# Inverting the 16x16 diagonal blocks of the delta rule from 4x4 and 8x8 blocks instead of row by row

## The chip, the cores and the metric

The kernel is one program on one core of a Trainium2 chip. The metric is the device time of one execution in microseconds (us); less is better. The engines are named as the profile names them: PE is TensorE (matrix products), DVE is VectorE, ACT is ScalarE, POOL is GpSimd, and SP issues most DMAs.

## The reference, cut to what matters

The program is a first block of two layers, followed by a second block that the change does not touch. A layer adds a feed-forward network, a mixer and another feed-forward network to x. The mixer has three parts: attention over selected keys, RWKV-7 time mixing, and a gated delta rule. The last two are recurrences over the 512 tokens. The reference writes the delta rule in chunks of 64 tokens with a triangular solve:

```
for l in range(DEPTH):                                   # DEPTH = 2
    x = x + 0.5 * swiglu(rms_norm(x, ...), ...)
    p = rms_norm(x, mix_norm[l]) @ w_in[l]
    pa, pb, pc = split_cols(p, GROUP_SPLITS)
    ya = dsa_attention(pa, ...)                          # top-k keys of each query, softmax
    yb, v_first = rwkv7_time_mix(pb, ...)                # 4 heads
    yc = gated_deltanet(pc, ...)                         # 4 heads
    x = x + jnp.concatenate([ya, yb, yc], axis=-1) @ w_out[l]
    x = x + 0.5 * swiglu(rms_norm(x, ...), ...)

# inside gated_deltanet, for each head and each chunk of 64 tokens
lower = jnp.where(strict, einsum('bhncd,bhnsd->bhncs', kb, k) * decay, 0.0)
rhs = jnp.concatenate([v * beta[..., None], kb * jnp.exp(g)[..., None]], axis=-1)
sol = lax.linalg.triangular_solve(eye + lower, rhs, left_side=True, lower=True, unit_diagonal=True)
```

RWKV-7 is written as a scan over tokens in the reference; the kernel gives it the same chunked form with the same solve.

## The kernel before, in words

Each layer's mixer is built by `Mix.__init__`. The projections (tiles `pf`, three matmuls for each fp32 product) feed everything. Four parts then run the chunked recurrence, each for two heads: `r0` and `r1` (RWKV) and `g0` and `g1` (gated delta rule). Each calls `Mix.core()` once, so a layer has four calls and the program eight. Attention stands beside them: the selection of keys (`index`, lines 542 to 544, repeated MAX8 and MATCH_REPLACE on DVE), and `att(t)` for the four tiles t of 128 queries. `att(t)` first rotates the queries (L471, L473) and turns and splits them (`qs`, L486). Then come two groups of four heads. For each head there are two matmuls, a masked maximum on DVE (L612), an exponential on ACT (L617) and a reciprocal (L619). After four heads the weights are turned by PE (`pT`, copied by L626) and multiplied by the values. L633 copies the tile's result out. `att(3)` has the widest scores, 128x512.

The order on each engine is not the order of the code. A scheduler lays out all instructions by streams with a tag and a level (`chain("c", 0)`, `("a", 0)` for the recurrences, `("g", 1)` for attention, `("x", 1)` for the selection, `("w", 2)` for weights); each engine then works through its own queue strictly in that order. The mixer ends with the product by `w_out`, which takes its eight pieces in the order 4, 5, 6, 7 (the recurrences), 0, 1, 2, 3 (attention).

`core()` solves the 64x64 triangular systems in two levels. The blocks G (`GA` for the delta rule, written by L1053) go to DRAM (L654), and their 16x16 diagonal blocks come back with one block on each of 64 partitions (L655): tile `d16`, 256 numbers each. GpSimd sets the identity in `x16`. Then 15 steps follow the rows of the block. Step s multiplies column s below the diagonal with row s of the inverse so far (L663, (15-s)(s+1) numbers) and adds that to all rows below (L665). Each of the 30 instructions needs the one before it. L666 copies the transposed inverse beside it, L667 writes both to DRAM, L672 reads them back in the layout of the 128-partition tiles, and L676 spreads them into block-diagonal tiles X0 and XT0. PE then multiplies (`lv`, L691), with DVE additions (`v`, L701) between the products, `WU` (L709), `qg` (L720), the matrices M (L745) and the eight states S (L759), whose result the part turns into `y` and `yo` (for g0 and g1: L1069, L1071).

Of the kernel before, what the change touches and what calls it, by code (L numbers as in the profile page):

```python
# [14 lines left out]
ALU = mybir.AluOpType  # L15
AX = mybir.AxisListType
# [76 lines left out]
def bc(ap, shape):  # L93
    return ap.to_broadcast(shape)
# [233 lines left out]
class Mix:  # L328
# [310 lines left out]
    def core(self, G, R, KH, RT, PC, extra=None, beta=None):  # L639
# [3 lines left out]
        nc, n, sm = self.nc, self.n, self.sm  # L643
# [5 lines left out]
        dt = n.f("d16")[:64]  # L649
        d16, t16 = dt[:, 0:256].rearrange("p (s t) -> p s t", s=16), dt[:, 256:320]  # L650
# [2 lines left out]
            for e in range(2):  # L653
                q.dma_start(out=rows[th, e], in_=G[th][e][:, :, 0:128])  # L654
        q.dma_start(out=d16, in_=s1[:, 0:2048].rearrange("x (s t) -> x s t", t=128)[:, :, 0:16])  # L655
        x16 = n.f("x16")[:64].rearrange("p (a c) -> p a c", a=2)
        X = x16[:, 0].rearrange("p (r c) -> p r c", r=16)
        nc.gpsimd.memset(x16[:, 0], 0.0)
        nc.gpsimd.memset(x16[:, 0, 0:256:17], 1.0)
        for s in range(15):  # L660
            a, m = 15 - s, s + 1
            tt = t16[:, :a * m].rearrange("p (r c) -> p r c", r=a)
            nc.vector.tensor_mul(out=tt, in0=bc(d16[:, s, s + 1:16].rearrange("p (r o) -> p r o", o=1), [64, a, m]),  # L663
                                 in1=bc(X[:, s:s + 1, 0:m], [64, a, m]))
            nc.vector.tensor_add(out=X[:, s + 1:, 0:m], in0=X[:, s + 1:, 0:m], in1=tt)  # L665
        nc.vector.tensor_copy(out=x16[:, 1].rearrange("p (c r) -> p c r", c=16), in_=X.rearrange("p r c -> p c r"))  # L666
        q.dma_start(out=s2.rearrange("a p c -> p a c"), in_=x16)  # L667
        xs2 = n.f("xs16")
        m16 = n.c("m16").rearrange("p (o g c) -> p o g c", o=1, g=8)
        xs = [xs2[:, a * 128:(a + 1) * 128].rearrange("p (i c) -> p i c", i=8) for a in range(2)]  # L670
        for a in range(2):
# [27 lines left out]
        for _ in range(3):  # L699
            w = self.half("v") if v is R else v  # L700
# [7 lines left out]
        else:  # L708
            prod(XT0, v, lambda h, b: nc.vector.tensor_mul(  # L709
                out=WU[h].rearrange("p (u e) c -> p u e c", e=2), in0=b.rearrange("p (u e) c -> p u e c", e=2),  # L710
                in1=bc(beta[:, 2 * h:2 * h + 2], [128, 2, 2, 128])))

        blocks = [(th, u, e) for th in range(2) for u in range(2) for e in range(2)]
# [14 lines left out]
        for cp in range(2):  # L728
            cs = slice(cp * 64, cp * 64 + 64)
            b = n.bank("bMB")  # L730
            col = lambda a, th, u: slice(a * 256 + (th * 2 + u) * 64, a * 256 + (th * 2 + u) * 64 + 64)
# [3 lines left out]
            for th, u, e in blocks:  # L735
                i = th * 4 + 2 * u + e
# [17 lines left out]
        for c in range(1, 8):  # L754
            nc.tensor.matmul(bY[:, c * 64:c * 64 + 64], lhsT=st(c), rhs=RT[:, c * 64:c * 64 + 64], start=False, stop=(c == 7))
            if c < 7:
                b = n.bank("bS")
# [832 lines left out]
```

## Time and the profile before

| | |
|---|---|
| time, median of 3 runs | 3542.82 us (3540.81 to 3544.31) |
| profiled execution, its time and its span | 3542.9 us, 3541.1 us |
| PE busy | 3414.4 us, 96% of the span |
| DVE busy | 2010.9 us, 57% |
| ACT busy | 1274.9 us, 36% |
| mixer of layer 0, layer 1 | about 375 to 801 us, 1560 to 1990 us |

The span runs from the first to the last instruction of the profiled execution; the 1.8 us between it and that execution's time lie around the program. Busy shares are means over very different stretches: in the feed-forward networks PE has no gap to speak of, and in the last 150 us of each mixer no engine is busy throughout.

### The profile page before, as it was taken

To read this page: it belongs to the slowest core of one execution; us is meant where nothing else is said; L and a number is where in the kernel's file an instruction comes from. 1 tells how busy PE (TensorE), PEld (TensorE's weight loads), DVE (VectorE), ACT (ScalarE), POOL (GpSimd) and SP (SyncE) were. 2 spreads that over 40 slices of the span, in tenths; PEclk is the share of its full clock that TensorE was granted. 3 is DMA by queue.
4 is the path that set the end of the run, shared out by engine and by line. 5 is a ranking of instruction groups with operands and counts; after the bars stand their busy time and mean duration, and the time that the engine had idled before them with its cause. 6 is when DMAs were issued, how large, how long until landed. Compare 5 with 4: busy or idle time off the path is not lost.

```text
span 3541.1 us, 44468 instructions
## 1 busy us (share of the span) xinstructions
PE 3414.4 (96%) x17314; PEld 2801.3 (79%) x17314; DVE 2010.9 (57%) x4364; ACT 1274.9 (36%) x2060; POOL 84.7 (2%) x168
## 2 busy tenths in 40 slices
PE   8999999889999999999998899999999999989999
PEld 7888778668888888887877688888777888778887
DVE  5555688765555555559978555535785332473332
ACT  4332544453332233335344433324563222232321
POOL 0000010000000000001100000000000000000000
PEclk9999999789999999999978999999999999989999
DMA  5346321103335434552210233432202333223332
GB/s 164 119 140 210 112 66 50 30 16 115 123 122 190 152 119 122 192 156 65 52 49 14 84 115 124 131 110 79 78 7 83 96 100 97 69 78 99 97 95 95
DMA packets 329955, 355.73 MB, mean 100 GB/s; under 512 B 41192, under 2 KB 249480, under 8 KB 329616
## 3 DMA queue, kind: packets, MB, share of 16 engines
q1 hardware_dynamic: 328576, 351.03, 32.5%
q8 instruction: 136, 2.23, 0.3%
q10 hardware_dynamic: 1168, 1.85, 0.2%
q14 instruction: 75, 0.61, 0.1%
HBM read 338.68 MB, written 14.16 MB: 100 GB/s over the span
## 4 chain that ended last, share of the span: by engine, by line
PE 89%; DVE 7%; ACT 2%; issue 1%; DMA 1%; POOL 0%; SPq 0%; DVEq 0%; ACTq 0%; POOLq 0%
PE pg L168 13%; PE pg L170 13%; PE pg L169 13%; PE pd L168 8%; PE pd L169 8%; PE pd L170 8%; PE pf L169 2%; PE pf L170 2%; PE pf L168 2%; PE lv L691 2%; PE G L904 1%; PE pt L430 1%; PE pt L431 1%; PE pt L429 1%; DVE wlo L162 1%
## 5 line engine op out<-in xcount | busy, mean ns | idle before, releaser
L162 DVE TENSOR_TENSOR wlo<-wraw,whi 128x1024 fp32r<-128x1024 f32 (+2 forms) x504 | 609.3, 1209 | 958.8 <-ACT whi L161 958.1
L161 ACT CAST whi<-wraw 128x1024 fp32r<-128x1024 f32 (+2 forms) x504 | 524.8, 1042 | 1283.6 <-PE pd L169 505.4
L168 PE MATMUL pg<-xh,whi 128*128 128x512 f32 x2112 | 825.5, 391 | 14.1 <-ACT whi L161 10.6
L170 PE MATMUL pg<-xh,wlo 128*128 128x512 f32 x2112 | 824.0, 390 | 0.0
L169 PE MATMUL pg<-xl,whi 128*128 128x512 f32 x2112 | 823.9, 390 | 0.0
L168 PEld LDWEIGHTS pg<-xh,whi 128*128 128x128 f32 x2112 | 398.1, 189 | 97.0 <-ACT whi L161 10.6
L169 PEld LDWEIGHTS pg<-xl,whi 128*128 128x128 f32 x2112 | 397.9, 188 | 83.1 <-DVE xl L273 0.6
L170 PEld LDWEIGHTS pg<-xh,wlo 128*128 128x128 f32 x2112 | 397.6, 188 | 83.5 <-DVE wlo L162 0.8
L168 PE MATMUL pd<-h,whi 128*128 128x512 f32 x1056 | 410.9, 389 | 0.0
L170 PE MATMUL pd<-h,wlo 128*128 128x512 f32 x1056 | 410.9, 389 | 0.0
L169 PE MATMUL pd<-h,whi 128*128 128x512 f32 x1056 | 410.8, 389 | 0.0
L1106 DVE CUSTOM_DVE_ANT_0 araw<-araw,act 128x512 f32<-128x512 f32 x224 | 148.9, 688 | 145.9 <-DMA araw<-in_ada_w_dram 140.6
L169 PEld LDWEIGHTS pd<-h,whi 128*128 128x128 f32 x1056 | 198.2, 188 | 41.3
L170 PEld LDWEIGHTS pd<-h,wlo 128*128 128x128 f32 x1056 | 198.2, 188 | 41.2
L168 PEld LDWEIGHTS pd<-h,whi 128*128 128x128 f32 x1056 | 198.2, 188 | 40.9
L168 PE MATMUL pf<-xh,whi 128*128 128x512 f32 (+4 forms) x424 | 167.0, 395 | 0.9 <-ACT xh L272 0.9
L169 PE MATMUL pf<-xl,whi 128*128 128x512 f32 (+4 forms) x424 | 167.3, 395 | 0.4 <-DVE xl L273 0.4
L170 PE MATMUL pf<-xh,wlo 128*128 128x512 f32 (+4 forms) x424 | 166.7, 393 | 0.0
L294 ACT ACTIVATE t<-t 128x512 f32<-128x512 f32 x88 | 55.6, 632 | 252.4 <-DVE t L293 250.6
L174 DVE TENSOR_TENSOR h<-t,h 128x512 fp32r<-128x512 f32 x132 | 90.8, 690 | 65.0 <-ACT h L173 64.7
L173 ACT CAST h<-t 128x512 fp32r<-128x512 f32 x132 | 81.8, 620 | 123.6 <-DVE t L296 76.7
L169 PEld LDWEIGHTS pf<-xl,whi 128*128 128x128 f32 (+2 forms) x424 | 79.1, 187 | 17.9 <-DVE xl L273 2.5
(494 smaller groups left out, 4692.8 us busy)
## 6 DMA issues: line engine op xcount, KB each, us to landing
wraw<-in_ffn_w_dram SPq DMA_DIRECT2D x132, 512.0 KB, 3.7
araw<-in_ada_w_dram SPq DMA_DIRECT2D x112, 512.0 KB, 3.5
wraw<-in_ffn_w_gate_dram SPq DMA_DIRECT2D x88, 512.0 KB, 3.8
wraw<-in_ffn_w_up_dram SPq DMA_DIRECT2D x88, 512.0 KB, 4.5
wraw<-in_ffn_w_down_dram SPq DMA_DIRECT2D x88, 512.0 KB, 3.6
wraw<-in_w_in_dram SPq DMA_DIRECT2D x69, 512.0 KB, 3.8
wraw<-in_w_out_dram SPq DMA_DIRECT2D x16, 512.0 KB, 3.5
xd<-x SPq DMA_DIRECT2D x24, 256.0 KB, 4.1
```

The costliest lines, as they stand in the source:

```text
L161: nc.scalar.copy(out=hi[:, :k * n], in_=raw[:, :k * n])
L162: nc.vector.tensor_sub(out=lo[:, :k * n], in0=raw[:, :k * n], in1=hi[:, :k * n].bitcast(F32))
L168: mm(out, lhsT=wh, rhs=xh, start=start, stop=False)
L169: mm(out, lhsT=wh, rhs=xl, start=False, stop=False)
L170: mm(out, lhsT=wl, rhs=xh, start=False, stop=stop)
L173: self.nc.scalar.copy(out=hi, in_=src)
L174: self.nc.vector.tensor_sub(out=lo, in0=src, in1=hi.bitcast(F32))
L294: nc.scalar.activation(out=t1, in_=t1, func=AF.Silu)
L429: mm(o, lhsT=self.xh[kk][:, ts], rhs=wh[:, k], start=s0, stop=False)
L430: mm(o, lhsT=self.xh[kk][:, ts], rhs=wl[:, k], start=False, stop=False)
L691: nc.tensor.matmul(b[:, i * 128:(i + 1) * 128], lhsT=lhs[th][:, i], rhs=rhs(th, i) if callable(rhs) else rhs[th][:, i], start=(i == 0), st ...
L1106: nc.vector.tensor_tensor_reduce(out=r[:, i], in0=r[:, i], in1=act, scale=1.0, scalar=0.0, op0=ALU.mult, op1=ALU.add, accum_out=acc[:, j + ...
```

## The change

The 16x16 unit triangular block is inverted from smaller blocks. First its four 4x4 diagonal blocks are inverted at once, by rows: a copy of the first column (L665) and two steps of a product and an addition (L669, L671). Then for k = 4 and k = 8 the block under the diagonal of each 2k x 2k block is filled with the product of three kxk matrices. A product of two kxk matrices is one elementwise product of k*k*k numbers (L679, L681), whose last axis is then summed (L680, L682, tensor_reduce). For k = 4 that is done for two blocks, for k = 8 for one. The products' scratch is the tile `xs16`, which takes the DMA's data afterwards. Instead of 30 instructions with 1360 numbers for each partition there are 17 with 2628 (12 and 56 in the 4x4 part, 512 for k = 4, 2048 for k = 8); the copy behind them (now L683) stays. All later lines of the file are 16 higher: L676 becomes L692, L745 becomes L761.

```
             for e in range(2):
                 q.dma_start(out=rows[th, e], in_=G[th][e][:, :, 0:128])
         q.dma_start(out=d16, in_=s1[:, 0:2048].rearrange("x (s t) -> x s t", t=128)[:, :, 0:16])
-        x16 = n.f("x16")[:64].rearrange("p (a c) -> p a c", a=2)
+        xt = n.f("x16")
+        x16 = xt[:64].rearrange("p (a c) -> p a c", a=2)
         X = x16[:, 0].rearrange("p (r c) -> p r c", r=16)
         nc.gpsimd.memset(x16[:, 0], 0.0)
         nc.gpsimd.memset(x16[:, 0, 0:256:17], 1.0)
-        for s in range(15):
-            a, m = 15 - s, s + 1
-            tt = t16[:, :a * m].rearrange("p (r c) -> p r c", r=a)
-            nc.vector.tensor_mul(out=tt, in0=bc(d16[:, s, s + 1:16].rearrange("p (r o) -> p r o", o=1), [64, a, m]),
-                                 in1=bc(X[:, s:s + 1, 0:m], [64, a, m]))
-            nc.vector.tensor_add(out=X[:, s + 1:, 0:m], in0=X[:, s + 1:, 0:m], in1=tt)
+
+        xs2 = n.f("xs16")
+        blocks = lambda t, k: t[:64, 0:272].rearrange("p (b w) -> p b w", b=16 // k)[:, :, 0:16 * k].rearrange("p b (r c) -> p b r c", c=16)
+        d, x = blocks(dt, 4), blocks(xt, 4)
+        nc.vector.tensor_copy(out=x[:, :, 1:4, 0], in_=d[:, :, 0, 1:4])
+        for s in (1, 2):
+            a, m = 3 - s, s + 1
+            tt = t16[:, :4 * a * m].rearrange("p (b r c) -> p b r c", b=4, r=a)
+            nc.vector.tensor_mul(out=tt, in0=bc(d[:, :, s, s + 1:4].rearrange("p b (r o) -> p b r o", o=1), [64, 4, a, m]),
+                                 in1=bc(x[:, :, s:s + 1, 0:m], [64, 4, a, m]))
+            nc.vector.tensor_add(out=x[:, :, s + 1:4, 0:m], in0=x[:, :, s + 1:4, 0:m], in1=tt)
+        for k in (4, 8):
+            for b in range(8 // k):
+                d, x = blocks(dt, 2 * k)[:, b], blocks(xt, 2 * k)[:, b]
+                tt = t16[:, b * k * k:(b + 1) * k * k].rearrange("p (r c) -> p r c", r=k)
+                m4 = xs2[:64, b * 64:b * 64 + k ** 3].rearrange("p (i j k) -> p i j k", i=k, j=k)
+                row = lambda t: bc(t.rearrange("p i (o k) -> p i o k", o=1), [64, k, k, k])
+                col = lambda t: bc(t.rearrange("p (o k) j -> p o j k", o=1), [64, k, k, k])
+                nc.vector.tensor_mul(out=m4, in0=row(d[:, 0:k, k:2 * k].rearrange("p k i -> p i k")), in1=col(x[:, 0:k, 0:k]))
+                nc.vector.tensor_reduce(out=tt, in_=m4, axis=AX.X, op=ALU.add)
+                nc.vector.tensor_mul(out=m4, in0=row(x[:, k:2 * k, k:2 * k]), in1=col(tt))
+                nc.vector.tensor_reduce(out=x[:, k:2 * k, 0:k], in_=m4, axis=AX.X, op=ALU.add)
         nc.vector.tensor_copy(out=x16[:, 1].rearrange("p (c r) -> p c r", c=16), in_=X.rearrange("p r c -> p c r"))
         q.dma_start(out=s2.rearrange("a p c -> p a c"), in_=x16)
-        xs2 = n.f("xs16")
         m16 = n.c("m16").rearrange("p (o g c) -> p o g c", o=1, g=8)
         xs = [xs2[:, a * 128:(a + 1) * 128].rearrange("p (i c) -> p i c", i=8) for a in range(2)]
         for a in range(2):
```

The scheduler's order changes with it, also far from the inverse. On DVE, the queue from an inverse's first to its last instruction held 31 of its own and 18 to 85 others; now it holds 18 of its own and 13 to 43 others.

The first place is DVE at the inverse of g1 in layer 1 (`x_15160` before and `x_15069` after are its tile x16; the lines with lv, v and XT are g0's products). Before:

```order
L665 TENSOR_TENSOR x_15160<-x_15160,d_15154 64x13x3
L663 TENSOR_TENSOR d_15154<-d_15154,x_15160 64x48
L665 TENSOR_TENSOR x_15160<-x_15160,d_15154 64x12x4
L663 TENSOR_TENSOR d_15154<-d_15154,x_15160 64x55
L701 TENSOR_TENSOR v<-lv,R 128x512
L665 TENSOR_TENSOR x_15160<-x_15160,d_15154 64x11x5
L663 TENSOR_TENSOR d_15154<-d_15154,x_15160 64x60
L701 TENSOR_TENSOR v<-lv,R 128x512
L665 TENSOR_TENSOR x_15160<-x_15160,d_15154 64x10x6
L701 TENSOR_TENSOR v<-lv,R 128x512
L663 TENSOR_TENSOR d_15154<-d_15154,x_15160 64x63
L676 TENSOR_TENSOR XT_14902<-xs_14839,cst 128x512
```

After, the same inverse, from its first instruction to its k = 4 part:

```order
L692 TENSOR_TENSOR XT_14812<-xs_14729,cst 128x512
L725 TENSOR_TENSOR WU<-lv,beta 128x512
L626 COPY pT<-pT 128x512
L665 COPY x_15069<-d_15063 64x4x3
L725 TENSOR_TENSOR WU<-lv,beta 128x512
L669 TENSOR_TENSOR d_15063<-d_15063,x_15069 64x16
L542 MAX m_12860<-acc 128x8
L671 TENSOR_TENSOR x_15069<-x_15069,d_15063 64x4x2x2
L543 MATCH_REPLACE acc<-m_12860,acc 128x512
L669 TENSOR_TENSOR d_15063<-d_15063,x_15069 64x12
L736 TENSOR_TENSOR qg<-bR,qg 128x512
L671 TENSOR_TENSOR x_15069<-x_15069,d_15063 64x4x3
```

Before, g0's products stand between the steps of g1's inverse; now all of g0's v and XT rows stand ahead of it, and rows of the key selection (MAX, MATCH_REPLACE) and of attention stand between.

The second place is DVE in layer 1 where g1's output is made (L1069 and L1071 before, L1085 and L1087 after). Before:

```order
L205 SCALAR_TENSOR_TENSOR rsy_15705<-rst_15706,rsy_15705 128x8
L486 TENSOR_TENSOR qs<-qT,qs 64x512
L1069 SCALAR_TENSOR_TENSOR y<-y,par_92,spr 128x512
L486 TENSOR_TENSOR qs<-qT,qs 64x512
L1071 TENSOR_TENSOR yo<-y,z 128x512
L612 ISA p,sx_15893<-s,msk 128x512
L612 ISA sx_15893 128x1
L612 ISA p,sx_15893<-s,msk 128x512
L612 ISA sx_15893 128x1
L616 SCALAR_TENSOR_TENSOR sx_15894<-sx_15893,qsc 128x1
```

After:

```order
L1085 SCALAR_TENSOR_TENSOR y<-y,par_92,spr 128x512
L626 COPY pT<-pT 128x512
L1087 TENSOR_TENSOR yo<-y,z 128x512
L612 ISA p,sx_15640<-s,msk 128x384
L612 ISA sx_15640 128x1
L174 TENSOR_TENSOR yl_15941<-oe,yh_15940 128x128
L616 SCALAR_TENSOR_TENSOR sx_15641<-sx_15640,qsc 128x1
L174 TENSOR_TENSOR yl_15941<-oe,yh_15940 128x128
L174 TENSOR_TENSOR yl_15951<-oe,yh_15950 128x128
L612 ISA p,sx_15640<-s,msk 128x384
L612 ISA sx_15640 128x1
L174 TENSOR_TENSOR yl_15951<-oe,yh_15950 128x128
```

Before, the heads behind `yo` are those of the last query tile (128x512), whose `qs` is ready; now they are the second four heads of the tile before it (128x384), and the rotation of the last tile's queries comes after those heads' pT copies:

```order
L626 COPY pT<-pT 128x512
L162 TENSOR_TENSOR wlo<-wraw,whi 128x1024 x2
L626 COPY pT<-pT 128x512
L471 TENSOR_TENSOR rpu<-qtm,ropet 128x8x32 x2
L473 TENSOR_TENSOR qtm<-qtm,rpu 128x512
L174 TENSOR_TENSOR yl_15941<-oe,yh_15940 128x128
L174 TENSOR_TENSOR yl_15951<-oe,yh_15950 128x128
L174 TENSOR_TENSOR yl_15961<-oe,yh_15960 128x128
L174 TENSOR_TENSOR yl_15971<-oe,yh_15970 128x128
L486 TENSOR_TENSOR qs<-qT,qs 64x512
L612 ISA p,sx_15789<-s,msk 128x512
```

In layer 0 the eight heads of tile 2 stand ahead of g1's `yo` in the new order, and the two pT copies of its second group and the rotation for tile 3 behind it; before, tile 3's `qs` stood ahead of that `yo` there as well.

The third place is DVE in layer 0 at the end of r1's inverse (`x_3715` is r1's x16, `X_4109` and `X_4110` are r0's X0). Before:

```order
L665 TENSOR_TENSOR x_3715<-x_3715,d_3709 64x2x14
L162 TENSOR_TENSOR wlo<-wraw,whi 128x1024
L663 TENSOR_TENSOR d_3709<-d_3709,x_3715 64x15
L544 TENSOR_SCALAR msk<-acc 128x256
L665 TENSOR_TENSOR x_3715<-x_3715,d_3709 64x15
L542 MAX m_3378<-acc 128x8
L666 COPY x_3715<-x_3715 64x256
L543 MATCH_REPLACE acc<-m_3378,acc 128x384
L542 MAX m_3381<-acc 128x8
```

After:

```order
L680 TENSOR_REDUCE d_3709<-xs_3718 64x64
L542 MAX m_3315<-acc 128x8
L681 TENSOR_TENSOR xs_3718<-x_3715,d_3709 64x512
L692 TENSOR_TENSOR X_4109<-xs_4087,cst 128x512
L692 TENSOR_TENSOR X_4110<-xs_4087,cst 128x512
L682 TENSOR_REDUCE x_3715<-xs_3718 64x8x8
L412 TENSOR_TENSOR pz<-pf,rstd 128x512
L683 COPY x_3715<-x_3715 64x256
L162 TENSOR_TENSOR wlo<-wraw,whi 128x1024
L717 TENSOR_TENSOR v<-lv,R 128x512
```

Before, nothing of r0's products stood ahead of r1's copy; now r0's two X0 expansions, which need r0's transfer through DRAM, stand ahead of the last reduction and of the copy of r1.

On ACT the new order has 37 loads of activation tables instead of 31; the new ones stand at L617, L971 and L1061, in the part of each mixer that prepares g0 and g1.

## Rows read from the trace of the kernel before

**Rows 1.** The page: span, busy time of the engines, chain that ended last.
```profile
span 3541.1 us, 44468 instructions
...
PE 3414.4 (96%) x17314; PEld 2801.3 (79%) x17314; DVE 2010.9 (57%) x4364; ACT 1274.9 (36%) x2060; POOL 84.7 (2%) x168
...
PE 89%; DVE 7%; ACT 2%; issue 1%; DMA 1%; POOL 0%; SPq 0%; DVEq 0%; ACTq 0%; POOLq 0%
```

**Rows 2.** Stretches: length; busy us (count) of PE, PEld, DVE, ACT, POOL; PEclk; DMA.
```profile
525.00:550.00 25.00, 24.15 (x186) 22.89 (x185) 24.72 (x59) 5.03 (x7) 1.98 (x3) 1.00 0.40 85
694.80:721.20 26.40, 23.00 (x212) 19.79 (x210) 23.61 (x80) 9.07 (x25) 4.66 (x6) 0.86 0.05 9
721.20:772.30 51.10, 46.63 (x354) 38.63 (x355) 35.05 (x107) 22.92 (x53) 4.16 (x6) 0.90 0.04 6
772.30:801.00 28.70, 22.78 (x102) 13.58 (x100) 15.06 (x52) 18.77 (x41) 0.00 (x0) 0.76 0.22 67
1882.40:1908.80 26.40, 21.33 (x188) 17.47 (x187) 20.99 (x68) 7.48 (x20) 4.68 (x6) 0.81 0.12 19
1908.80:1960.90 52.10, 46.80 (x368) 38.89 (x369) 36.12 (x109) 23.83 (x56) 4.16 (x6) 0.91 0.04 6
1960.90:1989.50 28.60, 23.11 (x105) 14.22 (x104) 15.16 (x51) 18.32 (x40) 0.00 (x0) 0.81 0.21 62
```

**Rows 3.** Groups by shape: busy us, mean ns of one, idle before.
```profile
L663 DVE TENSOR_TENSOR d<-d,x 64x15 f32<-64x15 f32 x16 | 2.6, 161 | 0.7 <-DMA d<-s 0.5
...
L663 DVE TENSOR_TENSOR d<-d,x 64x64 f32<-64x64 f32 x8 | 1.7, 209 | 0.0
...
L676 DVE TENSOR_TENSOR X<-xs,cst 128x512 f32<-128x512 f32 x16 | 10.4, 682 | 1.7 <-DMA xs<-s 1.5
...
L583 DVE TENSOR_REDUCE qss<-qsq 128x8 f32<-128x512 f32 x8 | 5.2, 679 | 0.5 <-ACT qsq L582 0.5
...
L971 ACT ACT_TABLE_LOAD x2 | 2.6, 1283 | 0.0
```

**Rows 4.** Timeline of DVE, inverse of g1 in layer 1 and what follows it.
```profile
1881.67 0.68 DVE L1053 TENSOR_TENSOR GA<-G,DD 128x512 f32<-128x512 f32 x1
...
1890.35 0.17 DVE L663 TENSOR_TENSOR d<-d,x 64x15 f32<-64x15 f32 x1 [0.53 <-DMA d<-s]
1890.55 0.18 DVE L665 TENSOR_TENSOR x<-x,d 64x15 f32<-64x15 f32 x1
...
1908.40 0.37 DVE L666 COPY x<-x 64x256 f32<-64x256 f32 x1
...
1916.18 0.68 DVE L676 TENSOR_TENSOR X<-xs,cst 128x512 f32<-128x512 f32 x1
```

**Rows 5.** Timeline of DVE, first inverse of layer 0 and its X0.
```profile
524.71 0.20 DVE L663 TENSOR_TENSOR d<-d,x 64x48 f32<-64x48 f32 x1
524.83 0.37 DVE L666 COPY x<-x 64x256 f32<-64x256 f32 x1
...
533.28 0.68 DVE L676 TENSOR_TENSOR X<-xs,cst 128x512 f32<-128x512 f32 x1
```

**Rows 6.** Timeline of DVE, end of Mix in layer 1: attention and g1's output.
```profile
1938.45 0.54 DVE L612 CUSTOM_DVE_ANT_0 p<-s,msk 128x384 f32<-128x384 f32 x1
...
1944.03 0.56 DVE L612 CUSTOM_DVE_ANT_0 p<-s,msk 128x384 f32<-128x384 f32 x1 [0.39 <-PE s L611]
...
1951.72 0.69 DVE L626 COPY pT<-pT 128x512 f32<-128x512 f32 x1 [0.59 <-PE pT L436]
...
1952.40 0.42 DVE L471 TENSOR_TENSOR rpu<-qtm,ropet 128x256 f32<-128x256 f32 x1
...
1960.20 0.69 DVE L1071 TENSOR_TENSOR yo<-y,z 128x512 f32<-128x512 f32 x1
...
1960.92 0.69 DVE L612 CUSTOM_DVE_ANT_0 p<-s,msk 128x512 f32<-128x512 f32 x1
...
1987.14 0.69 DVE L626 COPY pT<-pT 128x512 f32<-128x512 f32 x1 [3.41 <-PE pT L436]
```

## The prediction

> **What bounds the kernel now.** I read the page first. PE is busy for 96% of the span, and the chain that ended last lies on PE for 89% and on DVE for 7% [rows 1]. In most of the program an engine other than PE can become a little slower or faster without effect. The change touches DVE, which is busy for 57%, and only inside the two mixers. So the second view is the busy time by stretch there. While projections still run, PE has hardly a gap: 24.15 of 25 us between 525 and 550, although DVE is full too (24.72) [rows 2]. After the projections it is different. I cut the end of each mixer at events of DVE: the last GA of g1, the end of the copy behind g1's inverse, g1's `yo`, and the end of attention. The three stretches take 26.4, 51.1 and 28.7 us in layer 0 and 26.4, 52.1 and 28.6 us in layer 1 [rows 2]. In none of them is an engine busy throughout: in the last one PE works 22.78 and DVE 15.06 of 28.7 us, at a granted clock of 0.76 of full speed, so between the two levels of 1.2 and 2.4 GHz [rows 2]. There the time is set by chains of dependent instructions, and by what stands ahead of them in DVE's queue. That is where the change can be worth something. The time is forecast from the profiled execution, 3542.9 us (3541.1 of span and 1.8 around it); the median of the runs, 3542.82, is the same.
>
> **The inverse itself.** A small DVE operation takes 161 ns with 15 numbers per partition and 209 with 64, one with 512 takes 682 [rows 3]. Of the 17 new ones, five have 12 to 16 numbers (5 x 0.16), eight read 64 (8 x 0.21) and four read 512 (4 x 0.68): 5.2 us of durations. The 30 old ones have 15 to 64; at a mean of about 0.2 they make 6.1 us. Run alone, one behind the other, the inverse gets about 1 us shorter. On a full DVE another price holds: an independent operation starts before the former has ended (524.71 + 0.20 is 524.91, the next starts at 524.83 [rows 5]). With 0.08 hidden in each, 30 x 0.08 = 2.4 us go off before and 17 x 0.08 = 1.4 after: 3.7 us before, 3.8 after, and nothing is won. No row shows a reduction over the last axis of 64x512; the nearest one, 128x512, takes 679 ns, as long as a product (682) [rows 3]. I take that, since it reads and writes the same number of elements; if strides through the small blocks cost twice as much, it is 4 x 0.68 = 2.7 us more for an inverse, and at the least it is nothing more.
>
> The Trainium skill ("VectorE: DVE Perf Modes", Rules for kernel authors) calls `tensor_reduce` the slowest DVE operation and advises against it on a hot path; the row above shows it no slower than a product here. The same section says to minimize the count of operations, which speaks for the change; the fixed cost in its errata section (58 cycles plus one per element at 0.96 GHz) gives 3.2 us for the old inverse and 3.8 for the new, an estimate from that page, +0.5 us each or +4 us for eight.
>
> So by the rows the new arithmetic is worth between -1 us and nothing for each of eight inverses (+2.7 at the strides' bound). What moves the time is the order.
>
> **Inverses of r0 and r1.** They lie under the projections, with PE busy for 24.15 of 25 us [rows 2]. r0's copy to its X0 takes 533.28 - 525.20 = 8.1 us, the trip through DRAM [rows 5]. In layer 0 the two X0 operations now stand ahead of r1's last reduction and copy, so that DVE waits for r0's data with r1's inverse behind it. I expect r0 done some 4 us earlier and r1 one or two later. Cover: PE's projections. Without the cover it costs up to 3 us, and it could also gain 1. I take +1 for both layers together.
>
> **g1's inverse.** From the last GA to the end of g1's copy 26.4 us pass in both layers [rows 2]. In layer 1 the first 8.0 of them are the trip through DRAM (1882.35 to 1890.35), the other 18.4 the inverse [rows 4]. Back to back its steps start 0.20 us apart [rows 4], so 30 of them would need some 6.5 us; the rest is g0's v, WU and M between them, each of which waits for PE. In the new order v and XT stand ahead. What stands between first and copy is some selection and attention (16 rows): I add the durations to 8 to 9 us. So 26.4 becomes about 17: -9 in each layer. Bounds: -3 if g0's products still keep DVE waiting ahead of the inverse, -12 if only the inverse itself counts (8.0 + 6). GA itself comes some 1 us later in layer 0, where two more us of DVE work stand ahead of it.
>
> **From that copy to g1's yo.** The chain (X0 7.4 us behind the copy [rows 4], products, M, S) is the same, 51 to 52 us now [rows 2]. In layer 1 there is about 2 us less DVE work between; in layer 0 two more, for tile 2's heads. I take 0 and -2, bounds +2 and -5.
>
> **What then comes late: attention.** After g1's `yo` the kernel before goes straight on with the last tile's heads (yo 1960.20, head 1960.92) [rows 6]. The new order has more left there. In layer 0 it is the end of tile 2's second group and the rotation for tile 3: from the fourth head to the end of the second pT copy 1944.03 to 1952.41 = 8.4 us, less 1.4 for the two instructions of `yo`, is 7.0; from the rotation to the first head 1952.40 to 1960.92 = 8.5 us, less the time that `yo` takes in it and a wait for it, 6.7 [rows 6]. Together 13.7. In layer 1 the whole group is left (1938.45 to 1952.41 = 14.0), with the rotation 20.7 [rows 6]. These are upper bounds, since the chains were timed with g1's S steps between them. The lower ones are the DVE work alone that the order puts behind `yo`, 3.7 and 6.6 us more than before. That stretch waits by latency (its last pT copy waited 3.41 us for PE [rows 6]), so I go nearer the upper ones: +10 and +15.
>
> **Table loads.** Six more at 1283 ns [rows 3] on ACT, which is busy for 36% [rows 1]. They stand where k, q and v of the delta rule are made, partly on the way to g0. From 0 to 7.7; I take +1.5.
>
> **Sum.** r0 and r1 +1; layer 0: +1 - 9 + 0 + 10 = +2; layer 1: -9 - 2 + 15 = +4; tables +1.5. That is +8.5: 3542.9 + 8.5 = 3551.4, forecast 3551.
>
> **Rivals.** 0.2% of this kernel, 7 us, is about what a measurement can tell from no change.
>
> *Faster.* g1's chain sets the end of the mixer, and the attention left behind costs only its DVE work: layer 0 +1 - 9 + 3.7 = -4.3, layer 1 -9 - 2 + 6.6 = -4.4, nothing upstream: about -9, 3534. With -12 in place of each -9 it reaches 3528. For it: every end-of-mixer stretch has idle DVE (15.06 of 28.7 us [rows 2]) that could take the work. Against it: that time is idle because each head waits for PE and ACT. It decides if the delayed groups add less than 9 us in layer 0 and 11 in layer 1.
>
> By the skill's page named above, fewer operations in a chain are a gain by themselves. That alone would be 8 x -1 us by the durations above, inside this rival's range.
>
> *No change.* Gain and loss in each layer meet: -8 + 8 and -11 + 11, the rest hidden: 3543, from 3536 to 3550. For it: the same attention and the same recurrences have to be done, with total DVE work equal within 1 us at the end of each mixer.
>
> *Much slower.* The upper bounds hold: +13.7 and +20.7 instead of 10 and 15, and the X0 wait of r1 (3) and the tables (5) are not hidden: +8.5 + 9.4 + 5.5 = +23, 3566. For it: PE has few projections left by then. Against it: PE was full around r1.
>
> **How the numbers follow.** Slower as forecast 0.34, much slower 0.10, no change 0.28, faster 0.28. The forecast's own range is 3550 to 3560. With the faster case to its -12 and the much slower one nearly whole, 3529 to 3567 leaves out about 0.1 at the low end and 0.05 above. Faster by over 0.2%: 0.28; within: 0.28; slower: 0.44.
>
> **What would show it.** In the changed profile: four products of 64x512 and reductions of 64x512 near 0.68 us; from g1's last GA to its copy about 17 us in place of 26.4; g1's `yo` 8 to 11 us earlier after that GA; and then from `yo` to the end of attention 39 us in layer 0 and 44 in layer 1 in place of 28.7 and 28.6. In layer 0 DVE should wait 2 to 3 us for the transfer ahead of r0's X0. The prediction is wrong if the last tile's heads start as soon after `yo` as before, or if the granted clock in these stretches changes, since longer gaps lower it and denser work could raise it; that is not in my sum.

## The result, and the profile after

The changed kernel took 3575.18 us in the median of five executions (3562.49 to 3585.84), the kernel before 3542.82 beside it (3539.62 to 3544.31). The ratio is 1.0085, interval 1.0055 to 1.0114: slower, by about 30 us. The direction was forecast, the size was not: 3551 with a range up to 3567.

The page's lines on span, busy time and chain, of the changed kernel, as in [rows 1]:

```profile
span 3573.4 us, 44393 instructions
...
PE 3429.6 (96%) x17314; PEld 2803.0 (78%) x17314; DVE 2016.7 (56%) x4260; ACT 1283.9 (36%) x2066; POOL 83.5 (2%) x168
...
PE 88%; DVE 7%; ACT 2%; issue 2%; DMA 1%; POOL 0%; SPq 0%; DVEq 0%; ACTq 0%; POOLq 0%
```

The span is 32.3 us longer, PE is busy for 15 us more with the same 17314 matmuls, and DVE for 6 us more. So part of the loss is PE taking longer for the same work, the rest is PE waiting.

The same stretches as in [rows 2], cut at the same events (columns as there), layer 0 and then layer 1:

```profile
709.95:728.26 18.31, 12.26 (x120) 8.91 (x119) 14.79 (x45) 4.12 (x12) 2.80 (x5) 0.88 0.07 12
728.26:780.53 52.27, 47.88 (x363) 38.01 (x364) 37.77 (x124) 24.67 (x61) 4.25 (x6) 0.86 0.04 6
780.53:824.55 44.02, 32.06 (x131) 17.80 (x129) 20.86 (x58) 22.41 (x47) 1.29 (x1) 0.75 0.13 43
1902.71:1919.12 16.41, 12.37 (x139) 9.44 (x137) 14.85 (x45) 2.86 (x8) 3.27 (x5) 0.98 0.07 13
1919.12:1974.88 55.76, 48.98 (x350) 38.75 (x352) 33.26 (x103) 20.66 (x53) 4.24 (x6) 0.79 0.04 6
1974.88:2023.29 48.41, 33.48 (x144) 18.87 (x144) 22.58 (x75) 27.04 (x58) 1.26 (x1) 0.75 0.12 38
```

From g1's last GA to the end of its copy 26.4 us have become 18.3 and 16.4. From there to g1's `yo` 51.1 and 52.1 have become 52.3 and 55.8. The last stretch, attention behind `yo`, has grown from 28.7 and 28.6 to 44.0 and 48.4. The three together are 8.2 and 12.8 us longer than before (to the same event, the end of the last copy of attention, the last stretches before are 28.8 and 29.2 us).

DVE in layer 1 at g1's inverse, timeline of the changed kernel, which answers to [rows 4]:

```profile
1902.03 0.68 DVE L1069 TENSOR_TENSOR GA<-G,DD 128x512 f32<-128x512 f32 x1
...
1908.53 0.16 DVE L665 COPY x<-d 64x12 f32<-64x12 f32 x1
1908.72 0.69 DVE L725 TENSOR_TENSOR WU<-lv,beta 128x512 f32<-128x512 f32 x1
1909.33 0.16 DVE L669 TENSOR_TENSOR d<-d,x 64x16 f32<-64x16 f32 x1
1909.41 0.68 DVE L542 MAX8 m<-acc 128x8 f32<-128x512 f32 x1
...
1911.78 0.69 DVE L736 TENSOR_TENSOR qg<-bR,qg 128x512 f32<-128x512 f32 x1 [0.83 <-PE bR L734]
...
1918.75 0.37 DVE L683 COPY x<-x 64x256 f32<-64x256 f32 x1
```

Between the steps stand WU, the selection (MAX8) and one wait of 0.83 us for PE at `qg`; the chain of g0's products no longer does. The copy ends 16.4 us behind the GA. In the kernel before, g0's products brought waits for PE between the steps, the longest here:

```profile
1893.83 0.69 DVE L701 TENSOR_TENSOR v<-lv,R 128x512 f32<-128x512 f32 x1 [1.51 <-PE lv L691]
```

DVE behind g1's `yo` in layer 1, timeline of the changed kernel, which answers to [rows 6]:

```profile
1974.20 0.68 DVE L1087 TENSOR_TENSOR yo<-y,z 128x512 f32<-128x512 f32 x1
1974.80 0.55 DVE L612 CUSTOM_DVE_ANT_0 p<-s,msk 128x384 f32<-128x384 f32 x1
...
1986.01 0.68 DVE L626 COPY pT<-pT 128x512 f32<-128x512 f32 x1
1986.61 0.75 DVE L471 TENSOR_TENSOR rpu<-qtm,ropet 128x256 f32<-128x256 f32 x2
1988.73 0.69 DVE L473 TENSOR_TENSOR qtm<-qtm,rpu 128x512 f32<-128x512 f32 x1 [1.38 <-POOL qtm L472]
...
1992.79 0.69 DVE L612 CUSTOM_DVE_ANT_0 p<-s,msk 128x512 f32<-128x512 f32 x1 [1.32 <-PE s L611]
...
2020.83 0.69 DVE L626 COPY pT<-pT 128x512 f32<-128x512 f32 x1 [3.42 <-PE pT L436]
```

Behind `yo` come four heads of 384 columns, their pT copies, the rotation, a wait of 1.38 us for POOL, and only some 18 us after `yo` the first head of the last tile (1974.80 to 1992.79), which before came at once. The last pT copy waits 3.42 us for PE, as before (3.41).

In layer 0 the last tile's first head starts 11.75 us after `yo`. Stretches from `yo` to that head and from there to the end of attention (columns as in [rows 2]):

```profile
780.53:792.28 11.75, 11.21 (x53) 7.22 (x51) 8.78 (x20) 6.55 (x17) 1.29 (x1) 0.94 0.14 47
792.28:824.54 32.26, 20.85 (x78) 10.58 (x78) 12.08 (x38) 15.86 (x31) 0.00 (x0) 0.68 0.13 41
```

In the kernel before, the head starts at once, and from it to the end of attention in layer 0:

```profile
772.39:801.19 28.80, 22.69 (x101) 13.51 (x99) 15.00 (x51) 18.96 (x41) 0.00 (x0) 0.76 0.23 69
```

The other part of the loss lies earlier. Busy time of the changed kernel around 490 to 530 us (columns as in [rows 2]; the granted clock is the third number from the end):

```profile
490.00:500.00 10.00, 10.00 (x32) 6.60 (x31) 6.17 (x14) 0.58 (x1) 1.14 (x3) 0.59 0.22 63
500.00:510.00 10.00, 10.00 (x33) 5.81 (x33) 4.31 (x8) 0.74 (x2) 2.33 (x5) 0.50 0.30 82
510.00:520.00 10.00, 10.00 (x37) 6.39 (x38) 3.87 (x13) 1.12 (x3) 2.42 (x7) 0.50 0.07 7
520.00:530.00 10.00, 10.00 (x41) 7.80 (x40) 5.88 (x24) 2.71 (x6) 0.00 (x0) 0.54 0.07 7
```

And of the kernel before:

```profile
490.00:500.00 10.00, 10.00 (x37) 7.04 (x36) 6.47 (x15) 0.96 (x2) 1.14 (x3) 0.66 0.18 54
500.00:510.00 10.00, 10.00 (x63) 6.16 (x62) 7.48 (x17) 1.60 (x5) 4.76 (x12) 1.00 0.35 85
```

PE is busy in all of these stretches; around 491 us it works on the products G of r0 and r1, with transposes between them. There the granted clock falls to 0.5 of full speed (1.2 GHz) in both kernels. In the kernel before it is back at 1.00 some 7 us later; in the changed kernel's profile it stays low until about 529 us. On every engine, the order of the two kernels is the same up to the first instruction of the first inverse, which comes at 510 us before. What began at 491 us is therefore not the work of an instruction that the change touched. Whether the length of the drop is chance or comes from the change in some other way was the first question to the chip.

To compare kernels I cut each profile at three events in a layer: the first product G of the recurrences, `y` of r1 (DVE L937), and the first product of the next network. All in us:

| kernel | layer 0: G to y | y to next network | layer 1: G to y | y to next network | ratio to before, interval |
|---|---|---|---|---|---|
| before | 174.0 | 175.9 | 174.8 | 172.0 | 1 |
| changed | 190.0 | 182.4 | 170.0 | 187.6 | 1.0085 (1.0055 to 1.0114) |
| e1 old order | 187.9 | 175.9 | 175.0 | 172.5 | 1.0003 (0.998 to 1.0025) |
| e2 r0, r1 only | 171.0 | 171.5 | 170.0 | 169.1 | 0.9995 (0.9969 to 1.0022) |
| e3 g0, g1 only | 177.1 | 181.3 | 174.0 | 179.4 | 1.0024 (1.0003 to 1.0045) |
| e4 changed, attention 2, 3 first | 175.4 | 172.8 | 170.6 | 178.9 | 0.9981 (0.996 to 1.0002) |
| e5 changed again | 189.8 | 182.5 | 171.3 | 186.9 | 1.0069 (1.0041 to 1.0097) |
| e6 before, attention 2, 3 first | 168.1 | 168.0 | 175.0 | 174.1 | 1.001 (0.9986 to 1.0034) |
| e7 r only, attention 2, 3 first | 188.6 | 175.6 | 170.0 | 180.7 | 1.0046 (1.0025 to 1.0067) |
| e8 changed, numbers kept | 190.1 | 179.8 | 170.0 | 177.5 | 1.005 (1.0029 to 1.0071) |
| e9 e8 and attention 2 first | 181.2 | 176.4 | 171.5 | 169.5 | 0.9987 (0.9964 to 1.001) |
| e10 r only, attention 2 first | 191.9 | 163.9 | 171.2 | 166.1 | 0.9964 (0.9943 to 0.9986) |

The stage times are of one profile each; the ratios are of 5 to 12 executions of a kernel and 5 to 35 of the kernel before beside it. The drop near 491 us is long (34 to 38 us) in the profiles of the changed kernel, e1, e5, e7, e8 and e10, short (7 to 10 us) in those of the kernel before, e3, e4 and e9, and absent in e2 and e6.

### The profile page after: what moved, and what is told of

Read it like the earlier page. It is cut to its first block, busy times and chain, and to the rows that moved or that the text cites. A ratio compares the mean times of both kernels' runs of the same rounds, so it can differ in the third digit from the quotient of the medians.

```text
span 3573.4 us, 44393 instructions
## 1 busy us (share of the span) xinstructions
PE 3429.6 (96%) x17314; PEld 2803.0 (78%) x17314; DVE 2016.7 (56%) x4260; ACT 1283.9 (36%) x2066; POOL 83.5 (2%) x168
## 4 chain that ended last, share of the span: by engine, by line
PE 88%; DVE 7%; ACT 2%; issue 2%; DMA 1%; POOL 0%; SPq 0%; DVEq 0%; ACTq 0%; POOLq 0%
PE pg L168 13%; PE pg L170 13%; PE pg L169 13%; PE pd L168 8%; PE pd L169 8%; PE pd L170 8%; PE pf L170 2%; PE pf L169 2%; PE pf L168 2%; PE lv L707 2%; PE G L920 1%; PE o L1384 1%; PE o L628 1%; PE spr L791 1%; PE pt L430 1%
```

## The experiments

**e1 to e5: is the drop of the clock the change's, and which half of the change costs?**

e1 keeps the old inverse and only allocates `xs16` earlier, which leaves each engine's order as before:

```
+        xs2 = n.f("xs16")
         for s in range(15):
...
-        xs2 = n.f("xs16")
```

> The old inverse by rows, with the tile xs16 only allocated where the changed kernel allocates it; every engine's order is that of the kernel before. Theory A (the order behind g1's output costs the time, and the long drop of the granted clock around 490 to 530 us in layer 0 is chance, since it began ahead of the first changed instruction): 3543, with some executions 10 to 20 us longer at a lower mean clock. Theory B (that drop belongs to the change, through the tile's place or the new order): 3543 in all executions, mean clock 0.965, none longer.

Measured: 3553.3 us (3540.3 to 3566.6), ratio 1.0003 (0.998 to 1.0025). Its profile at the place in question:

```profile
490.00:500.00 10.00, 10.00 (x31) 6.45 (x31) 6.00 (x13) 0.59 (x1) 1.15 (x3) 0.60 0.19 54
500.00:510.00 10.00, 10.00 (x32) 5.79 (x32) 4.05 (x8) 0.74 (x2) 2.33 (x5) 0.50 0.32 92
520.00:530.00 10.00, 10.00 (x40) 7.70 (x40) 4.47 (x15) 2.34 (x6) 0.00 (x0) 0.52 0.07 7
```

The long drop is there, with the old inverse and the old order, at 0.50 until about 529 us. e1 does have the tile where the changed kernel has it; but the kernel before, without that, went from 3532 to 3569 us in its 35 executions beside this run, at mean clocks of 0.972 to 0.957. The long drop does not need the change, and theory B falls as it was put. Whether the change makes it more frequent is another question; e5 bears on it.

e2 and e3 use the new inverse for one kind of part and the loop over rows for the other:

```
+        if beta is None:          # e2: r0 and r1;  e3: if beta is not None, g0 and g1
...
+        else:
+            for s in range(15):
```

> The new inverse for r0 and r1 only, the old one for g0 and g1. Theory A: the end of both mixers is as before, so 3540 to 3547 where the clock does not drop in layer 0 (mean clock 0.965) and about 13 more where it does. Theory B: the loss of about 14 us in the first r part is there in every execution, 3555 to 3560.

Measured: 3552.1 us, 0.9995 (0.9969 to 1.0022). The absolute numbers expected were too low for this comparison, in which the kernel before has 3552.5; by the ratio nothing is lost. The profiled execution is the shortest of the twelve (3521.3 us), and it has no drop near 491 us, although r0 and r1 have the new inverse:

```profile
490.00:500.00 10.00, 9.82 (x48) 6.39 (x47) 8.84 (x19) 0.96 (x2) 2.01 (x4) 1.00 0.30 85
```

Three more executions lie at 3534 to 3536 us with a mean clock of 0.971, the other eight at 3552 to 3565 with 0.961 to 0.964. Theory B's loss in every execution is not there. In layer 1 the r part is 4.8 us shorter.

> The new inverse for g0 and g1 only, the old one for r0 and r1. Four heads fewer than in the changed kernel are left behind g1's output in layer 1 (8 instead of 12). Theory A: most of the 19 us that the changed kernel's shortest execution has lost, so 3553 to 3562 at a mean clock of 0.965. Theory B: at most 3551.

Measured: 3559.1 us, 1.0024 (1.0003 to 1.0045). The absolute time is inside theory A's numbers, but those were made for a kernel before at 3543; by the ratio it is 8.5 us (1 to 16), which lies between the two theories. At the mean clock that theory A names it fits: at 0.965 to 0.967 the executions took 3551 to 3561 us, those of the kernel before beside it 3541 to 3550. The stages are clearer. From y on it is 5.4 and 7.4 us longer than the kernel before, so the new inverse of g0 and g1 alone brings most of the change's loss in layer 0 (6.5) and half of that in layer 1 (15.6).

e4 changes nothing in the arithmetic of the changed kernel. It puts attention tiles 2 and 3 into a stream that the scheduler prefers:

```
-        with chain("g", 1):
+        with chain("g", 0):
             self.att(2, "x", "pj")
-        with chain("g", 1):
+        with chain("g", 0):
             self.att(3, "x", "pj")
```

> The changed kernel with attention tiles 2 and 3 in a stream of level 0 instead of 1, so that behind g1's output 1 head is left in layer 0 and 5 in layer 1, instead of 8 and 12 in the changed kernel. Theory A (attention left behind sets the end): the last stretch of each mixer gets 12 to 18 us shorter than in the changed kernel, g1's output comes 3 to 8 us later; 3535 to 3545. Rival C (what is moved ahead delays g1's chain by as much): no more than 5 us below the changed kernel, 3557 to 3575.

Measured: 3544.9 us (3536.3 to 3559.1), 0.9981 (0.996 to 1.0002), at theory A's upper end. From g1's copy to `yo`, and from `yo` to the end of attention, layer 0 and then layer 1:

```profile
713.30:789.80 76.50, 66.06 (x436) 48.83 (x437) 50.66 (x158) 36.53 (x85) 5.58 (x7) 0.84 0.03 5
789.80:799.80 10.00, 10.00 (x58) 6.89 (x56) 6.73 (x23) 8.61 (x23) 0.00 (x0) 1.00 0.20 59
1896.10:1966.70 70.60, 59.84 (x402) 46.88 (x403) 43.54 (x136) 29.49 (x72) 5.39 (x7) 0.81 0.03 5
1966.70:1991.80 25.10, 19.48 (x92) 12.13 (x90) 12.87 (x41) 17.20 (x40) 0.00 (x0) 0.86 0.17 57
```

The last stretch went from 44.0 to 10.0 and from 48.4 to 25.1 us, more than expected; the stretch ahead of `yo` grew by 24.2 and 14.8, also more than expected. So well over half of the gain is given back ahead of `yo`, as rival C has it, but not all: the balance is -9.8 and -8.5. With the arithmetic unchanged, where `yo` stands against attention decides over most of what the mixers' ends had lost. And the clock at 500 us in this kernel with the whole new inverse:

```profile
490.00:500.00 10.00, 10.00 (x34) 6.51 (x33) 6.29 (x17) 0.59 (x1) 1.14 (x3) 0.66 0.19 54
500.00:510.00 10.00, 10.00 (x62) 6.55 (x64) 8.15 (x19) 1.49 (x4) 3.64 (x10) 1.00 0.38 98
```

It is back at 1.00 as early as in the kernel before.

e5 is the changed kernel once more.

> The changed kernel once more, beside the kernel before on the chip of the other experiments. Theory A: 18 to 22 us over the kernel before at the same mean clock, that is a ratio of 1.005 to 1.006, with both kernels spread over 30 us by the clock; the ratio of 1.0085 held executions of the kernel before that had no long drop. Theory B (the drop of the clock belongs to the change): a ratio of 1.0085 or more, and a mean clock lower by 0.004 or more than the kernel before has on this chip.

Measured: 3575.0 us against 3548.6, ratio 1.0069 (1.0041 to 1.0097), median of the mean granted clocks 0.961 against 0.9645. The ratio lies between the two theories and its interval holds both, and the clock is nearly as much lower as theory B asks; alone this run decides nothing. Its stages repeat those of the first profile to 1.3 us, the long drop included. About 0.003 of the lower clock belongs to the long last stretches: 92 us at 0.75, where before there were 57 at 0.76 and 0.81 (0.25 x 92.4 - 0.24 x 28.7 - 0.19 x 28.6 = 10.8 us of 3573). What is left, under 0.001, is all that the clock shows of a more frequent long drop; with so few executions that stays open. A profile shows one execution, so the long drops of the others cannot be counted.

**e6 to e10: is attention behind `yo` the cost whatever the inverse, and what would be better than both?**

e6 has the old inverse, e7 the new one for r0 and r1 only, both with e4's two lines.

> The kernel before, old inverse, with attention tiles 2 and 3 at level 0: no heads are left behind g1's output in either layer. If attention behind g1's output is what sets the end whatever the inverse, it gains 3 to 8 us on the kernel before. If what is moved ahead only delays g1's chain by as much (rival C), 0 within 3 us.

Measured: 3550.0 us, 1.001 (0.9986 to 1.0034). No gain can be told, which fits rival C; a gain of up to 5 us is still inside the interval. In the profile of this kernel attention ends 7 and 18 us ahead of `yo`, so with the old inverse and these two lines it is not what comes last. Its y to the next network is 7.9 us shorter in layer 0 and 2.1 longer in layer 1.

> New inverse for r0 and r1 only, attention tiles 2 and 3 at level 0: no heads behind g1's output. Theory A: at most the time of the new inverse for r0 and r1 alone, and 3 to 10 us below the kernel before, ratio 0.997 to 0.999. Rival C: the ratio of that experiment, 0.9995, or over.

Measured: 3564.5 us, 1.0046 (1.0025 to 1.0067). Theory A's numbers are missed, rival C's hold. From g1's copy to `yo` in the profile, both layers:

```profile
737.20:809.30 72.10, 61.68 (x419) 46.67 (x419) 39.20 (x125) 35.64 (x86) 4.36 (x6) 0.86 0.13 34
1927.20:2001.50 74.30, 63.30 (x437) 47.94 (x436) 40.64 (x131) 37.47 (x93) 4.36 (x6) 0.85 0.12 33
```

That is 72 and 74 us, where the kernel before has 51 and 52. Attention is done 17.5 and 17.7 us ahead of `yo`, so g1 is now what comes last. From `yo` to the next network it then takes 40.3 and 39.9 us, where from the end of attention the kernel before takes 33.2. "Attention first" is no rule: what is moved ahead holds up g1.

e8 keeps the changed kernel's inverse, but raises the scheduler's counter behind it, as if there were still 30 instructions:

```
                 nc.vector.tensor_reduce(out=x[:, k:2 * k, 0:k], in_=m4, axis=AX.X, op=ALU.add)
+        self.n.tc.cur_priority += 13
```

> The changed kernel with 13 added to the scheduler's priority number behind each inverse, so that all later instructions have the numbers that 30 instructions would give them; 8 heads are left behind g1's output in both layers, where the changed kernel has 8 and 12. Theory A: layer 0 as in the changed kernel, layer 1's last stretch 6 to 10 us shorter, so 6 to 10 us below the changed kernel. If only the inverse's own length and not the numbers moves attention: the changed kernel's time within 4 us.

Measured: 3565.3 us, 1.005 (1.0029 to 1.0071), some 7 us less than e5 by the ratios, whose intervals overlap. The last stretch of layer 1:

```profile
1971.30:2009.70 38.40, 27.75 (x120) 15.66 (x118) 19.90 (x58) 21.22 (x45) 1.29 (x1) 0.82 0.16 47
```

It is 38.4 us, 10.0 below the changed kernel, with 8 heads behind `yo` instead of 12; in layer 0 it is 42.2 instead of 44.0. From y to the next network layer 1 takes 177.5 us in place of 187.6. So 13 missing instructions moved later ones by their numbers alone, and that was 10 of the 15.6 us that layer 1 had lost. The ratio itself, some 18 us over the kernel before, is more than the stages of this one profile explain without the long drop (+3.9 and +5.5 from y on, -4.8 in the r part of layer 1); what the other executions lose was not profiled.

e9 is e8 with attention tile 2 (not 3) at level 0, e10 is e2 with the same.

> The changed kernel with both measures: 13 added to the priority number behind each inverse, and attention tile 2 (not tile 3) at level 0. Behind g1's output 4 heads are left in both layers. Theory A: from layer 1's y to the first product of the next network 172 to 176 us (187 in the changed kernel, 172 before), in layer 0 170 to 176 (182 and 176); 3540 to 3547, a ratio to the kernel before of 0.997 to 1.000. Rival C (what is moved ahead delays g1 as much): a ratio of 1.003 or more.

Measured: 3545.0 us, 0.9987 (0.9964 to 1.001), y to the next network 176.4 and 169.5. The time is inside theory A's numbers, layer 0 is 0.4 us over them and layer 1 2.5 us better. Rival C's ratio is excluded: together the two measures give back the change's loss.

> New inverse for r0 and r1 only, attention tile 2 at level 0: 2 heads left behind g1's output in layer 0 and 4 in layer 1, where the new inverse for r0 and r1 alone leaves 6 and 8. Theory A: the same or up to 5 us below that experiment, a ratio of 0.996 to 0.9995. Rival C: above it, a ratio of 1.001 to 1.005, since g1's chain with the old inverse stands behind more attention.

Measured: 3532.5 us (3520.4 to 3545.4) against 3544.3, 0.9964 (0.9943 to 0.9986): by 0.4% faster than the kernel before, inside theory A's numbers. Against e2 (0.9995) the intervals overlap, so what tile 2 alone brings is less sure. The last stretch of both layers:

```profile
795.70:806.40 10.70, 9.51 (x52) 5.90 (x52) 7.44 (x26) 9.25 (x23) 0.00 (x0) 1.00 0.17 45
1972.70:1987.20 14.50, 12.62 (x69) 9.03 (x68) 10.01 (x33) 11.71 (x27) 0.00 (x0) 1.00 0.17 57
```

Attention and g1's `yo` now end within 11 and 15 us of each other, at a granted clock of 1.00. From y to the next network it takes 163.9 and 166.1 us, the least of all kernels tried, although its profile has the long drop and the longest first r part (191.9).

## Why the prediction was wrong in size

Two steps failed. The term for attention that comes late was sized too low, +10 and +15 against +15.2 and +19.2 measured; and the granted clock, which the text named as a risk at the ends of the mixers alone, stood in the sum at nothing, where the long drop under r0 and r1 costs 13.9 us. A smaller miss is the way from g1's copy to `yo`. The sum misses the time by 23.8 us: 13.9 are the long drop, 9.4 attention, 6.9 the way to `yo`; the r parts without the drop (-3.7), the table loads (-1.5) and smaller differences elsewhere (-1) take some of it back. Without the long drop the time would have been near 3561, inside the range.

**The bound.** That the time is made at the end of the mixers, by what stands ahead of what in DVE's queue, held: there the changed kernel loses 6.5 and 15.6 us from y to the next network. The full account by the table: before the first G +1.0, layer 0 G to y +16.0, y to next network +6.5, on to layer 1's G -1.1, G to y -4.8, y to next network +15.6, the rest -0.9; together +32.3.

**The inverse itself** was priced too low by 0.8 us. New operations by shape, in the changed kernel:

```profile
L681 DVE TENSOR_TENSOR xs<-x,d 64x512 f32<-64x512 f32 x8 | 8.7, 1094 | 0.0
...
L679 DVE TENSOR_TENSOR xs<-d,x 64x512 f32<-64x512 f32 x8 | 8.1, 1018 | 0.0
...
L680 DVE TENSOR_REDUCE d<-xs 64x64 f32<-64x512 f32 x8 | 5.4, 670 | 0.0
...
L682 DVE TENSOR_REDUCE x<-xs 64x64 f32<-64x512 f32 x8 | 5.4, 669 | 0.0
...
L679 DVE TENSOR_TENSOR xs<-d,x 64x64 f32<-64x64 f32 x16 | 3.6, 250 | 0.0
...
L680 DVE TENSOR_REDUCE d<-xs 64x16 f32<-64x64 f32 x16 | 2.9, 201 | 0.0
```

The reductions take 670 ns, as forecast from the nearest row, but the products of 64x512 take 1018 and 1094 and not 682. The durations of all 17 add up to 6.0 us an inverse instead of 5.2; those of the 30 old ones to 6.2. So the arithmetic alone gains 0.1 us, inside the bounds given, and decides nothing. The warning of the Trainium skill ("VectorE: DVE Perf Modes", Rules for kernel authors) that `tensor_reduce` is the slowest operation is not borne out by these rows: the product was the slow one.

**Inverses of r0 and r1, +1 in all.** The feared wait is not there. DVE at the end of r1's inverse in layer 0:

```profile
535.79 0.37 DVE L683 COPY x<-x 64x256 f32<-64x256 f32 x1
...
541.14 1.10 DVE L681 TENSOR_TENSOR xs<-x,d 64x512 f32<-64x512 f32 x1
542.17 1.28 DVE L692 TENSOR_TENSOR X<-xs,cst 128x512 f32<-128x512 f32 x2
543.37 0.67 DVE L682 TENSOR_REDUCE x<-xs 64x64 f32<-64x512 f32 x1
```

r0's copy ends at 536.16, its X0 starts at 542.17 directly behind the product before it. What was missed is a gain: in layer 1 the r part takes 170.0 to 171.5 us in all eight profiles with the new inverse for r0 and r1, and 174.0 to 175.0 in the four with the old one. I had held it hidden under PE's projections; 4 us of it are not. In layer 0 there is a small loss instead, where profiles with the same drop are compared, new inverse against old: 171.0 and 168.1 without a drop (e2, e6; r0's copy comes 3.0 us earlier and r1's 1.2 later, near what the text expected), 175.4 and 174.0 with a short one (e4, before), 190.0 and 187.9 with a long one (changed, e1). Together the r parts are worth some -3 and not +1, apart from the drop.

**g1's inverse, -9 in each layer.** Right: -8.1 and -10.0. The inverse of g0 and g1 alone does it (e3 has 17.3 and 15.8 us), and since the durations of the inverse differ by only 0.1 us, it is the order, as stated, with g0's products ahead of it. GA itself, for which the sum had +1 in layer 0, comes 1.7 us earlier behind r1's `y` there and 2.9 later in layer 1.

**From the copy to yo, 0 and -2.** Too low: +1.2, inside the bounds, and +3.7, beyond them and of the other sign. The granted clock there was 0.86 and 0.79 where the kernel before had 0.90 and 0.91 [rows 2]. It is not shown to be the cause: e8 takes 53.1 and 55.8 us for this way at 0.90 and 0.91. The cause stays open.

**What then comes late, +10 and +15.** This is the step that failed within the sum. The place and the mechanism were right, as e4, e8 and e9 show; the size was not: it measured +15.2 and +19.2. In layer 1, 18.0 of that are the time to the first head of the last tile (my upper bound was 20.7), and 1.2 the heads themselves. I had gone below the upper bound on the thought that DVE's free time would take some of it. It did not: the steps on the way wait for PE, POOL or ACT. In layer 0 it was 11.7 to the first head and 3.5 for slower heads (32.3 in place of 28.8 us, at a granted clock of 0.68 in place of 0.76), together above the bound of 13.7.

With these sizes the sum is +8.2 and +12.8 from GA to the end of attention in place of +1 and +4 (without GA's own +1). With GA's -1.7 and +2.9, the r parts at the same drop (-4.8 and +2.1) and the rest of the program (-1.0) this comes to some +18 or 3561, near the shortest execution of the changed kernel, 3562.5, whose mean clock of 0.965 is that of the kernel before.

**Table loads, +1.5.** Not seen. e2 has the six more loads too, and its layer 1 is 4.8 us shorter than before from the first G to y and 2.9 from there to the next network.

**The clock, which was not in the sum.** The text said that a change of the granted clock at the ends of the mixers would make it wrong, and gave it neither a price nor a chance; of the clock under the projections it said nothing. The other four executions have mean clocks of 0.960 and 0.957 and 12 to 23 us more. In the profile the first r part is 190.0 - 174.0 = 16.0 us longer. In e1, which has the old inverse and order, it is 187.9 - 174.0 = 13.9 us, so that much is the long drop, and the other 2.1 go with the new inverse. That lifts the time out of the range. The kernel before had looked steady, with three executions within 4 us ahead of the prediction and five within 5 us beside the result; beside the experiments it spread over 37 us. So the direction was right for the reason given, but 13.9 of the 32 us have another source, and that all five executions of the kernel before beside it lay at 3544 or below was luck.

**The rivals.** "Much slower" was the nearest, but for another extra term than it named: its two upper bounds add up to 34.4 us, as do the two terms measured, though one lies above its bound and the other below, and that is luck; the wait ahead of r1's last steps and the tables, its other 5.5 us, were not there. For the "faster" rival the text asks for less than 9 us in layer 0; by its own terms, +1 and -9, it is 8. Why the drop ends early in some executions and late in others was not settled: the first G comes at 484.1 to 486.0 us in all twelve profiles, and short and long drops lie mixed in that range (485.1 without a drop in e6 and with a long one in e8).

## What to carry to other kernels

A shorter chain of instructions also moves whatever the scheduler orders by count: before pricing the arithmetic, list what stands ahead of and behind the last chains in each queue, and price what is left behind at its latency, not at its engine time. Where two chains meet at the end, look at which comes last: pushing attention wholly first cost as much elsewhere or more (e6, e7), and moving one tile gave the best time (e10). Before a difference under 1% is explained, see how the unchanged kernel spreads, and compare stage by stage.

## What the runs showed of the hardware

An elementwise product of 64x512 with operands that step through 8x8 blocks and repeat along one axis took 1018 and 1094 ns, where 128x512 products take about 680 and the reductions over the same scratch 670. The 64x64 products for k = 4 took 250 ns, where the old 64x64 rows have 209 [rows 3].

The granted clock fell to 1.2 GHz near 491 us, between products of 64x256 and transposes of 128x128, with PE busy for 9.07 to 9.68 of the 10 us before 490 and for 10.00 of the 10 after. It came back after 7 us (before) or after 37 (e1), with the same order of instructions on every engine; in e2 and e6 it did not fall there. A difference of 0.005 in the mean granted clock goes with about 13 us of time among executions of one kernel (0.965 and 0.960: 3562.5 and 3574.5 to 3575.7 in the changed kernel).
